# Two plain f blocks per layer, seven rounds, 16-key blocks of 128 rows, and a last round by 320 and 192 tokens

## The chip, the core and the metric

The kernel runs on one core of one Trainium2 chip. TensorE multiplies matrices into PSUM; VectorE (DVE) and ScalarE (ACT) do elementwise work, GpSimd (POOL) too but without access to PSUM; SyncE (SP) issues most DMA transfers. The engines run side by side, each in its own fixed order, and wait for one another through semaphores. The metric is the device time of one execution in microseconds (us); shorter is better.

## What is computed

The reference is two layers of a decoder. 16 learned tokens stand before the 512 tokens of the input and are dropped at the end, so a layer works on 528 columns and the last one needs 512.

```python
def hybrid_layer(h, ...):
    xn = rmsnorm(h, attn_norm_g)
    proj = jnp.einsum('bld,dc->blc', xn, w_in)
    fq, fk, fv, flog, rq, rk, rv, rg = jnp.split(proj, SPLIT_POINTS, axis=-1)
    fox_out = fox_attention(fq, fk, fv, log_sigmoid(flog + b_fgate))  # 8 heads of 64, softmax
    ret = retention_chunkwise(rotate(rq), rotate(rk), rv)             # 4 heads of 128, decay
    ret_out = jax.nn.silu(rg) * head_groupnorm(ret, ret_gn_g)
    mix = jnp.concatenate([fox_out, ret_out], axis=-1)
    h = h + jnp.einsum('blc,cd->bld', mix, w_out)
    hn = rmsnorm(h, ffn_norm_g)
    ff = jax.nn.silu(jnp.einsum('bld,df->blf', hn, w_gate)) * jnp.einsum('bld,df->blf', hn, w_up)
    return h + jnp.einsum('blf,fd->bld', ff, w_down)
```

Two such layers (D 1024, DFF 2816) and a final rmsnorm give the output. All inputs are float32.

## The kernel before

Everything is kept transposed: 128 features on the partitions, tokens along the columns. `h` is eight tiles of 128 x 528. Each product of float32 matrices is made of three fp32r matmuls: high part by high part, high by low, low by high (`split`, L119; the weights' parts are whi and wlo or fwhi and fwlo, L168, L169, L798, L799). Weights arrive by SP in tiles of 128 x 1024 (raw, three buffers; fraw, two) and are split by ScalarE and VectorE, in the attention stage mostly by ScalarE and POOL.

**Order.** The plan is a list of small steps. TensorE executes exactly in list order (`manual_schedule`, L1128). For the other engines a scheduler fixes the order when the program is built: what stands earlier in the list goes first, what isn't ready lets later work pass. `tc.high_priority()` moves instructions ahead; `keep_in_program_order` holds one behind the instruction listed before it on its engine.

**Attention.** Keys stand in five blocks: four of 128 and one of 16 (`KOFF`, `KLEN`, L561). `transpose_into` (L376) turns blocks through TensorE. For the last block the kernel uses tiles of 16 rows: the value products in `fox_steps` (L530) and `ret_steps` (L674) contract over `kn = KLEN[j]` rows, and in layer 0 the block of the 16 leading queries is turned as a 16 x 16 tile (L385).

**Feed-forward.** DFF is 22 blocks f of 128. The first `PLAIN` of a layer are plain: a gate product and an up product, each eight steps over D. Every other f is a `Unit` (L817): gate and up together as seven block products in place of eight, over two halves of the tokens. It needs sums of weight blocks (L844, L845, L851, L857) and sums of input blocks, the four **x forms** (`x_forms`, L764: scratch tile S of two buffers, results th and tl). The list places the x forms at fixed steps after the stage begins (L1024); they are needed by the first unit's `middle` (L904). A unit runs head, middle, one down product, tail, another down product. The blocks f go in rounds (`ROUNDS`); the down products of a round are the fills of the next round's units, one pair of output tiles per unit, and what no unit took follows at the round's end. Each adds its sum to `h` (L952).

**The end.** In the last layer the last round's down products run over the first half of the tokens, then over the second (`HC`, 256 and 256 columns; L997 adds to `h`). `squares_last` (L309) sums the squares of `h`, `rstd` multiplies them by ones on TensorE and forms R, `scaled` (L1041) multiplies `h` by the norm's weight on ScalarE, and `final` (L1033) multiplies by R and sends the output.

Of the kernel before, what the change touches and what calls it, by code (L numbers as in the profile page):

```python
# [16 lines left out]
NK = D // 128  # L17
# [9 lines left out]
ROUNDS = ((0, 3), (3, 7), (7, 11), (11, 15), (15, 19), (19, 22))  # L27
PLAIN = 3
# [10 lines left out]
def hybrid_kernel(ctx, tc, x_t, w_in, w_fl, w_out, w_gate, w_up, w_down, vecs, b_fg, rope, decay, mask, ident, out_t):  # L39
# [27 lines left out]
    p_tiles, pm_tiles, vt_tiles, low_keys = [], [], [], []  # L67
    rot = {"pm": 0, "vt": 0}
# [12 lines left out]
    def enter_att(l):  # L81
        enter("att")
        low_keys[:] = [phase["att"].tile([128, T], F32R, name=f"kl{s}") for s in range(2)]
        for s, t in enumerate(low_keys):
            (nc.gpsimd if l else nc.vector).memset(t[64 * (1 - s):64 * (2 - s)].bitcast(F32), 0.0)
        for lst, n, shape in ((p_tiles, NBLK, [128, TP]), (pm_tiles, 2, [META, 128]), (vt_tiles, 1, [128, T])):
            lst[:] = [phase["att"].tile(shape, F32, name=f"pd{shape[1]}_{n}_{i}") for i in range(n)]

            for i, t in enumerate(lst):
                if lst is not vt_tiles:  # L90
                    z0 = META + 128 * (i + 1) if lst is p_tiles else META
                    (nc.gpsimd if l else nc.vector).memset(t[:, z0:z0 + 128 - META], 0.0)
# [165 lines left out]
    def col_rstd(parts, n, cols, rname):  # L258
# [4 lines left out]
        for i, s in enumerate(parts):  # L263
            for v, (c0, c1) in zip(views, cols):
                nc.tensor.matmul(v, ones, s[:, c0:c1], start=(i == 0), stop=(i == len(parts) - 1))
# [43 lines left out]
    def squares_last(st, cols):  # L309
# [9 lines left out]
        sh, sl = (fft(f"tl{i}", shape=(128, T)) for i in range(2))  # L319
        sq = tt("sq")  # L320
        nc.scalar.activation(sh[:, c], h[NK - 1][:, c], AF.Square)
        nc.vector.tensor_mul(sq[:, c], h[NK - 1][:, c], h[NK - 1][:, c])
        nc.vector.tensor_sub(sl[:, c], sq[:, c], sh[:, c].bitcast(F32))
        st["parts"] = parts + (sh, sl)
# [51 lines left out]
    def transpose_into(src, offs, parts=128, last=128):  # L376


        out = []
        for j0 in range(0, len(offs), 4):  # L380
            grp = offs[j0:j0 + 4]
            ps = psum_a()
            rows = last if j0 + len(grp) == len(offs) and len(grp) == 1 else 128
            for j, o in enumerate(grp):
                nc.tensor.transpose(ps[0:rows, 128 * j:128 * j + parts], src[:, o:o + rows], idt[0:parts, 0:parts])  # L385
            out.append((j0, len(grp), rows, ps[0:rows, 0:128 * len(grp)].rearrange("p (j q) -> p j q", j=len(grp))))
        return out

    def fox_dense(l, g, ly, real, st):
# [30 lines left out]
        def v_done(ps):  # L420
            vt = take(vt_tiles, "vt")
# [10 lines left out]
    def fox_steps(g, st, ly, real):  # L432
# [5 lines left out]
        def values():  # L438
            st["v"] = [at(f"vv{s}", shape=(128, 5, 128)) for s in range(2)]
            for j0, n, rows, p3 in transpose_into(st["vt"], KOFF, last=META):  # L440
                for s in range(2):
                    v = st["v"][s][0:rows, j0:j0 + n]
# [11 lines left out]
        def scores(s, b):  # L454
# [11 lines left out]
            for c0, c1 in segs:  # L466
# [8 lines left out]
                nc.vector.tensor_tensor_reduce(pt[:, c0:c1], sc[0:nq, 0:c1 - c0], bc[0:nq, c0:c1],  # L475
# [11 lines left out]
            pr = pt[:, 0:nk]  # L487
# [16 lines left out]
        def turn(s, b):  # L504
# [6 lines left out]
            for j0, n, _, p3 in transpose_into(info[s, b], [128 * j for j in range(b + 2)], nq):  # L511
                split(pth[:, j0:j0 + n, q0:q0 + nq], ptl[:, j0:j0 + n, q0:q0 + nq], p3[:, :, 0:nq])

        def product(s):
# [11 lines left out]
            for j in range(5):  # L526
                c0 = max(0, KOFF[j] - META)
                kn = KLEN[j]
                for i, pp in enumerate(pt):
                    nc.tensor.matmul(po[:, c0:SEQ], v[0:kn, j, :], pp[0:kn, j, META + c0:T],  # L530
# [33 lines left out]
    def ret_dense(l, hd, ly, real, st, which):  # L564
# [17 lines left out]
        def v_done(ps):  # L582
            vr = at("vr", F32)
# [15 lines left out]
    def ret_steps(l, hd, st, real):  # L599
# [5 lines left out]
        def values():  # L605
# [3 lines left out]
            for j0, n, rows, p3 in transpose_into(st["vr"], KOFF, last=META):  # L609
                mn = mean[0:rows, j0:j0 + n]  # L610
                nc.vector.tensor_reduce(mn, p3, axis=mybir.AxisListType.X, op=ALU.add)
                nc.vector.tensor_scalar_mul(mn, mn, -1.0 / 128.0)
                for j in range(n):
                    nc.scalar.activation(vh[0:rows, j0 + j], p3[:, j], AF.Identity, bias=mn[:, j])
                for j in range(n):
                    nc.vector.scalar_tensor_tensor(vl[0:rows, j0 + j], p3[:, j], mn[:, j],
                                                   vh[0:rows, j0 + j].bitcast(F32), ALU.add, ALU.subtract)
# [6 lines left out]
        def scores(grp):  # L624
# [32 lines left out]
            if full < used:  # L657
                split(sh[0:kn, full:used], sl[0:kn, full:used], sd[0:kn, full:used])
            kept["t", grp[0]] = (sh, sl)

        def product(grp):
# [5 lines left out]
            for j in grp:  # L667
                used, g0 = kept[j]
                sh, sl = kept["t", g0]
                q0 = q_start(j)  # L670
                qa = max(q0, META)
                kn = KLEN[j]
                for i, (a, b) in enumerate(((vh, sh), (vh, sl), (vl, sh))):
                    nc.tensor.matmul(po[:, qa - META:SEQ], a[0:kn, j, :], b[0:kn, used + qa - q0:used + T - q0],  # L674
# [48 lines left out]
    def ffn(l, st, real, last):  # L723
# [77 lines left out]
        def product(j, o, x, bank, fresh, final, n=HB, done=None):  # L801

            def chunk(k):
                def go():
# [4 lines left out]
                    for i, (a, b) in enumerate(((hi, xh), (hi, xl), (lo, xh))):  # L809
                        nc.tensor.matmul(bank()[:, 0:w], a[:, o + k, :], b, start=(fresh and k == 0 and i == 0),  # L810
# [182 lines left out]
        else:  # L993
# [39 lines left out]
    def final(st, c0, c1, pinned=NK):  # L1033
        r = st["R"][:, c0:c1].unsqueeze(1).broadcast_to([128, 2, c1 - c0])
        for k in range(0, NK, 2):
# [167 lines left out]
```

## Time and profile before

| | before |
|---|---|
| time, median of 3 runs (lowest to highest) | 1299.45 us (1298.94 to 1300.29) |
| the profiled execution: its time, its span | 1300.5 us, 1298.7 us |
| granted TensorE clock, mean | 0.995 |
| VectorE busy in it | 1004.4 us (77%) |
| ScalarE busy in it | 706.1 us (54%) |
| HBM read, written | 116.91 MB, 2.13 MB |

The span runs from the first to the last instruction; the execution's time has some 2 us around it. PE is TensorE's matmuls and PEld its weight loads, which overlap them. A row of a group or of the timeline names line, engine, operation, tiles (out<-in) and shape; an arrow in brackets names what ended the idle time before an instruction.

### The profile page before, as it was taken

The numbers are of one execution on the slowest core, as the hardware profiler recorded it, in microseconds if no ns is written. First come the engines' busy times: TensorE is split into PE (matmuls) and PEld (weight loads), VectorE is DVE, ScalarE is ACT, GpSimd is POOL, SyncE is SP. The second block draws the span as 40 slices with busy tenths as digits, with TensorE's granted clock in tenths as the row PEclk, the third lists the DMA queues.
The fourth block names the chain that finished last, engine by engine and source line by source line (L and its number), as shares of the span: only waits on it lengthen the run. The fifth ranks groups of instructions, "written<-read, shape, count | busy, mean of one in ns | idle before, by whom it ended". The sixth has DMA issues, their size and how long they took to land.

```text
span 1298.7 us, 23288 instructions
## 1 busy us (share of the span) xinstructions
PE 1271.5 (98%) x9326; PEld 1207.8 (93%) x9326; DVE 1004.4 (77%) x1823; ACT 706.1 (54%) x1277; POOL 192.2 (15%) x153
## 2 busy tenths in 40 slices
PE   8999999999999999999999999999999999999996
PEld 7999999999999999999998989888789999999995
DVE  7877756769887888887776767567899887888866
ACT  6767545667544444444466665457664444444444
POOL 3332334230000000000023323333200000000000
PEclk9999999999999999999999999999999999999998
DMA  5322222213333333332313222222223333333321
GB/s 198 108 80 66 88 85 66 74 49 125 106 96 98 98 98 98 98 98 82 118 55 115 74 82 83 74 84 72 93 82 118 114 98 98 98 98 104 107 66 65
DMA packets 45468, 120.54 MB, mean 93 GB/s; under 512 B 5376, under 2 KB 12032, under 8 KB 45360
## 3 DMA queue, kind: packets, MB, share of 16 engines
q1 hardware_dynamic: 45120, 118.90, 29.2%
q8 instruction: 73, 1.20, 0.4%
q0 software_dynamic: 96, 0.13, 0.1%
q14 instruction: 35, 0.29, 0.1%
q10 hardware_dynamic: 144, 0.02, 0.0%
HBM read 116.91 MB, written 2.13 MB: 92 GB/s over the span
## 4 chain that ended last, share of the span: by engine, by line
PE 86%; DVE 7%; ACT 5%; issue 1%; DMA 1%; POOL 0%; SPq 0%; DVEq 0%; ACTq 0%; POOLq 0%
PE psd L192 24%; PE psa L810 18%; PE psd L945 14%; PE psd L810 13%; PE psa L192 5%; PE psa L945 4%; PE psa L385 2%; PE psa L530 1%; PE psa L674 1%; PE psa L469 1%; PE psa L647 1%; DVE xl L291 1%; ACT whi L168 1%; DVE tq L575 1%; PE psa L347 1%
## 5 line engine op out<-in xcount | busy, mean ns | idle before, releaser
L169 POOL TENSOR_TENSOR wlo<-raw,whi 128x512 fp32r<-128x512 f32 x136 | 186.5, 1387 | 400.5 <-ACT whi L168 398.3
L192 PE MATMUL psd<-xh,whi 128*128 128x264 f32 (+1 forms) x792 | 197.0, 316 | 5.0 <-ACT whi L168 5.0
L192 PE MATMUL psd<-xh,wlo 128*128 128x264 f32 (+1 forms) x792 | 187.2, 304 | 0.4 <-POOL wlo L169 0.4
L192 PE MATMUL psd<-xl,whi 128*128 128x264 f32 (+1 forms) x792 | 187.1, 304 | 0.4 <-DVE xl L291 0.4
L192 PEld LDWEIGHTS psd<-xh,whi 128*128 128x128 f32 x792 | 128.8, 190 | 9.9 <-ACT whi L168 5.0
L192 PEld LDWEIGHTS psd<-xh,wlo 128*128 128x128 f32 x792 | 127.5, 189 | 6.5 <-POOL wlo L169 0.6
L192 PEld LDWEIGHTS psd<-xl,whi 128*128 128x128 f32 x792 | 128.1, 189 | 5.2 <-DVE xl L291 1.0
L168 ACT CAST whi<-raw 128x512 fp32r<-128x512 f32 (+1 forms) x170 | 99.4, 613 | 38.8 <-issue 19.8
L798 ACT CAST whi<-raw 128x1024 fp32r<-128x1024 f32 (+2 forms) x62 | 54.8, 884 | 49.6 <-PE psd L810 37.6
L798 ACT CAST fwhi<-raw 128x1024 fp32r<-128x1024 f32 (+2 forms) x62 | 55.7, 899 | 47.2 <-PE psd L810 39.4
L799 DVE TENSOR_TENSOR wlo<-raw,whi 128x1024 fp32r<-128x1024 f32 (+2 forms) x62 | 62.9, 1015 | 11.9 <-ACT whi L798 11.7
L799 DVE TENSOR_TENSOR fwlo<-raw,fwhi 128x1024 fp32r<-128x1024 f32 (+2 forms) x62 | 64.0, 1032 | 8.8 <-ACT fwhi L798 8.6
L488 ACT ACTIVATE pd<-pd,nmax 128x144 f32<-128x144 f32 (+4 forms) x72 | 39.3, 545 | 52.7 <-DVE nmax L475 40.8
L810 PE MATMUL psa<-tl,whi 128*128 128x264 f32 (+1 forms) x232 | 65.8, 284 | 0.0
L810 PE MATMUL psa<-th,whi 128*128 128x264 f32 (+1 forms) x232 | 65.8, 284 | 0.0
L810 PE MATMUL psa<-th,wlo 128*128 128x264 f32 (+1 forms) x232 | 65.7, 283 | 0.0
L810 PE MATMUL psa<-th,fwhi 128*128 128x264 f32 (+1 forms) x224 | 63.6, 284 | 0.0
L810 PE MATMUL psa<-th,fwlo 128*128 128x264 f32 (+1 forms) x224 | 63.5, 284 | 0.0
L810 PE MATMUL psa<-tl,fwhi 128*128 128x264 f32 (+1 forms) x224 | 63.4, 283 | 0.0
L121 DVE TENSOR_TENSOR ptl<-psa,pth 128x512 fp32r<-128x512 f32 (+4 forms) x88 | 41.8, 490 | 24.2 <-ACT pth L120 23.9
L798 ACT CAST fwhi<-S 128x1024 fp32r<-128x1024 f32 x20 | 21.0, 1051 | 69.7 <-PE psa L810 66.3
L876 ACT COPY e<-psa 128x264 f32<-128x264 f32 (+1 forms) x114 | 42.8, 375 | 27.9 <-PE psa L810 23.9
(291 smaller groups left out, 4030.8 us busy)
## 6 DMA issues: line engine op xcount, KB each, us to landing
raw<-w_in SPq DMA_DIRECT2D x54, 512.0 KB, 3.5
raw<-w_gate SPq DMA_DIRECT2D x44, 512.0 KB, 3.9
fraw<-w_up SPq DMA_DIRECT2D x38, 512.0 KB, 3.5
raw<-w_down SPq DMA_DIRECT2D x64, 256.0 KB, 2.9
raw<-w_out SPq DMA_DIRECT2D x16, 512.0 KB, 3.4
raw<-w_down SPq DMA_DIRECT2D x32, 192.0 KB, 2.5
bc<-cdr SPq DMA_DIRECT2D x16, 264.0 KB, 3.5
raw<-w_up SPq DMA_DIRECT2D x6, 512.0 KB, 3.6
```

The lines of the kernel that those rows point to most:

```text
L121: nc.vector.tensor_sub(lo, src, hi.bitcast(F32))
L168: nc.scalar.copy(hi, job["raw"][:, c0:c1])
L169: sub(lo, job["raw"][:, c0:c1], hi.bitcast(F32))
L192: nc.tensor.matmul(ps[1][b][:, 0:c1 - c0], w[:, wk, :], x[:, c0:c1], start=(k == 0 and i == 0), stop=(k == n - 1 and i == 2))
L291: nc.vector.scalar_tensor_tensor(xl[:, c], h[k][:, c], g, xh[:, c].bitcast(F32), ALU.mult, ALU.subtract)
L385: nc.tensor.transpose(ps[0:rows, 128 * j:128 * j + parts], src[:, o:o + rows], idt[0:parts, 0:parts])
L488: nc.scalar.activation(pr, pr, AF.Exp, bias=nmax[0:nq], scale=-1.0, accum_out=rsum)
L798: nc.scalar.copy(hi, src)
L799: nc.vector.tensor_sub(lo, src, hi.bitcast(F32))
L810: nc.tensor.matmul(bank()[:, 0:w], a[:, o + k, :], b, start=(fresh and k == 0 and i == 0), stop=(k == n - 1 and i == 2), skip_group_check= ...
L876: nc.scalar.copy(self.t["e"][:, i], self.t["x"][:, 0:w])
L945: nc.tensor.matmul(v[:, 0:c1 - c0], a[:, s * n + k, :], b[:, c0:c1], start=(k == 0 and i == 0), stop=(k == n - 1 and i == 2))
```

## The change

It has four parts.

1. `PLAIN` goes from 3 to 2, and the 22 blocks go in seven rounds (2, 4, 4, 3, 3, 3, 3) in place of six (3, 4, 4, 4, 4, 3). One more f of each layer is a unit.
2. The 16-key block is padded with zeros to 128 rows: two value tiles of 640 columns (`v_tiles`), the 16-query tiles of 128 rows (`pm_tiles`), and small tiles `end_tiles` for the retention block's scores, zeroed once when the attention stage of a layer is entered. Products and transposes of that block then use 128 rows.
3. The last round runs over 320 and then 192 columns. The first part's norm is now `squares`, the full one, and its `scaled` stands right behind its `rstd`.
4. `squares_last`, for the second part, sums six squares in place of seven, gives h6's square to TensorE as float32 without a split, and puts its additions ahead by priority. `final` and `scaled` are called in pieces with some of them pinned.

```diff
-ROUNDS = ((0, 3), (3, 7), (7, 11), (11, 15), (15, 19), (19, 22))
-PLAIN = 3
+ROUNDS = ((0, 2), (2, 6), (6, 10), (10, 13), (13, 16), (16, 19), (19, 22))
+PLAIN = 2
...
+        for lst, n, cols, z0 in ((p_tiles, NBLK, TP, None), (v_tiles, 2, TP, T)):
+            lst[:] = [phase["att"].tile([128, cols], F32, name=f"pd{z0}_{i}") for i in range(n)]
...
+        pm_tiles[:] = [phase["att"].tile([128, 128], F32, name=f"pm{i}") for i in range(2)] if l == 0 else []
+        for t in pm_tiles:
+            zero(l, t)
+        end_tiles[:] = [[phase["att"].tile([128, META], F32R, name=f"rs{i}{k}") for k in range(2)] for i in range(2)]
+        for t in end_tiles[0] + end_tiles[1]:
+            zero(l, t.bitcast(F32))
+
+    def zero(l, t):
+        (nc.gpsimd if l else nc.vector).memset(t, 0.0)
...
-                nc.tensor.matmul(v, ones, s[:, c0:c1], start=(i == 0), stop=(i == len(parts) - 1))
+                nc.tensor.matmul(v, ones if s.dtype == F32R else ones.bitcast(F32), s[:, c0:c1], start=(i == 0), stop=(i == len(parts) - 1))
...
-        for k in range(NK - 1):
+        for k in range(NK - 2):
             sq = tt("sq") if k else acc
             nc.scalar.activation(sq[:, c], h[k][:, c], AF.Square)
             if k:
-                nc.vector.tensor_add(acc[:, c], acc[:, c], sq[:, c])
-        parts = col_parts(acc, cols)
...
+                with tc.high_priority():
+                    nc.vector.tensor_add(acc[:, c], acc[:, c], sq[:, c])
+        hi, lo = col_parts(acc, cols)
+        one = fft("S", F32, (128, T), 2)
...
+        nc.scalar.activation(one[:, c], h[NK - 2][:, c], AF.Square)
         nc.scalar.activation(sh[:, c], h[NK - 1][:, c], AF.Square)
...
+        st["parts"] = (hi, one, lo, sh, sl)
...
-                nc.tensor.transpose(ps[0:rows, 128 * j:128 * j + parts], src[:, o:o + rows], idt[0:parts, 0:parts])
+                nc.tensor.transpose(ps[:, 128 * j:128 * j + 128], src[:, o:o + 128], idt)
...
-                    nc.tensor.matmul(po[:, c0:SEQ], v[0:kn, j, :], pp[0:kn, j, META + c0:T],
+                    nc.tensor.matmul(po[:, c0:SEQ], v[:, j, :], pp[:, j, META + c0:T],
...
+                eh, el = end_tiles[hd % 2]
+                split(eh[0:kn], el[0:kn], sd[0:kn, full:used])
...
+                if j == 4:
+                    (sh, sl), used = kept["e"], 0
                 for i, (a, b) in enumerate(((vh, sh), (vh, sl), (vl, sh))):
-                    nc.tensor.matmul(po[:, qa - META:SEQ], a[0:kn, j, :], b[0:kn, used + qa - q0:used + T - q0],
+                    nc.tensor.matmul(po[:, qa - META:SEQ], a[:, j, :], b[:, used + qa - q0:used + T - q0],
...
-            for c0, c1 in HC:
+            LC = ((t0, t0 + 320), (t0 + 320, T))
+            for c0, c1 in LC:
...
-            places = [(end, lambda: squares_last(fin[0], HC[0:1])),
-                      (end + 9, lambda: rstd(fin[0], HC[0:1], "r")),
-                      (2 * end, lambda: squares_last(fin[1], HC[1:2])),
-                      (2 * end, lambda: scaled(fin[1], *HC[1])),
-                      (2 * end, lambda: scaled(fin[0], *HC[0])),
-                      (2 * end, lambda: final(fin[0], *HC[0], NK // 2)),
-                      (2 * end, lambda: rstd(fin[1], HC[1:2], "R")),
-                      (2 * end, lambda: final(fin[1], *HC[1]))]
+            places = [(end, lambda: squares(fin[0], LC[0:1])),
+                      (end + 9, lambda: rstd(fin[0], LC[0:1], "r")),
+                      (end + 9, lambda: scaled(fin[0], *LC[0], 0, NK)),
+                      (2 * end, lambda: scaled(fin[1], *LC[1], 0, NK - 1)),
+                      (2 * end, lambda: squares_last(fin[1], LC[1:2])),
+                      (2 * end, lambda: final(fin[0], *LC[0], HB, NK)),
+                      (2 * end, lambda: scaled(fin[1], *LC[1], NK - 1, NK)),
+                      (2 * end, lambda: final(fin[0], *LC[0], 0, HB)),
+                      (2 * end, lambda: rstd(fin[1], LC[1:2], "R")),
+                      (2 * end, lambda: final(fin[1], *LC[1], 0, NK))]
...
+    def final(st, c0, c1, k0, k1):
...
+        for k in range(k0, k1, 2):
+            y = st["y"][k // HB][:, k % HB:k % HB + 2]
+            mul = nc.vector.tensor_mul(y, y, r)
+            if k0:
                 tc.keep_in_program_order(mul)
```

More of the change, by code (lines that the diff above doesn't have):

```diff
@@ L382, in transpose_into @@
             ps = psum_a()
[L383 removed]
             for j, o in enumerate(grp):
[L385 to L386 removed]
+                nc.tensor.transpose(ps[:, 128 * j:128 * j + 128], src[:, o:o + 128], idt)
+            out.append((j0, len(grp), ps[:, 0:128 * len(grp)].rearrange("p (j q) -> p j q", j=len(grp))))
         return out
@@ L420, in v_done @@
         def v_done(ps):
-            vt = take(vt_tiles, "vt")
+            vt = v_tiles[0]
             for t, (c0, c1) in zip(ps, FULL):
@@ L439, in values @@
             st["v"] = [at(f"vv{s}", shape=(128, 5, 128)) for s in range(2)]
-            for j0, n, rows, p3 in transpose_into(st["vt"], KOFF, last=META):
+            for j0, n, p3 in transpose_into(st["vt"], KOFF):
                 for s in range(2):
-                    v = st["v"][s][0:rows, j0:j0 + n]
+                    v = st["v"][s][:, j0:j0 + n]
                     a0, a1 = ROWS[s]
@@ L608, in values @@
             mean = tmp.tile([128, 5, 1], F32, name="mean", tag="mean")
-            for j0, n, rows, p3 in transpose_into(st["vr"], KOFF, last=META):
-                mn = mean[0:rows, j0:j0 + n]
+            for j0, n, p3 in transpose_into(st["vr"], KOFF):
+                mn = mean[:, j0:j0 + n]
                 nc.vector.tensor_reduce(mn, p3, axis=mybir.AxisListType.X, op=ALU.add)
@@ L809, in go @@
                     for i, (a, b) in enumerate(((hi, xh), (hi, xl), (lo, xh))):
-                        nc.tensor.matmul(bank()[:, 0:w], a[:, o + k, :], b, start=(fresh and k == 0 and i == 0),
+                        nc.tensor.matmul(bank()[:, 0:b.shape[-1]], a[:, o + k, :], b, start=(fresh and k == 0 and i == 0),
                                          stop=(k == n - 1 and i == 2), skip_group_check=not (fresh and final))
```

63 lines of the change are left out of this document (31 added, 32 removed).

## The prediction

> **What bounds the kernel now.** I read the head of the page first, then the busy time by windows, then single stretches of the timeline. In the page: the span, and the busy us of each engine with its share of it.
>
> ```profile
> span 1298.7 us, 23288 instructions
> ...
> PE 1271.5 (98%) x9326; PEld 1207.8 (93%) x9326; DVE 1004.4 (77%) x1823; ACT 706.1 (54%) x1277; POOL 192.2 (15%) x153
> ```
>
> TensorE is the bound, so an edit is worth the TensorE time it removes unless another engine then comes late. The windows (columns: stretch, length, busy us of PE, PEld, DVE, ACT, POOL, granted clock, DMA share, GB/s) show where one could:
>
> ```profile
> 60.00:90.00 30.00, 30.00 (x240) 29.42 (x240) 21.74 (x45) 21.36 (x43) 7.92 (x6) 1.00 0.29 88
> 315.00:330.00 15.00, 15.00 (x125) 14.84 (x124) 15.00 (x26) 8.40 (x12) 0.00 (x0) 1.00 0.24 66
> 400.00:500.00 100.00, 100.00 (x823) 100.00 (x822) 81.24 (x121) 43.23 (x61) 0.00 (x0) 1.00 0.32 99
> 955.00:970.00 15.00, 15.00 (x67) 12.19 (x66) 15.00 (x26) 8.23 (x12) 0.00 (x0) 1.00 0.32 98
> 1284.00:1299.00 15.00, 1.96 (x9) 1.28 (x7) 8.60 (x19) 3.22 (x9) 0.00 (x0) 0.63 0.40 138
> ```
>
> The attention stage (first row) has VectorE at 72%: TensorE alone decides. The feed-forward rounds (third) have VectorE at 81%. But at the **start of the feed-forward stage** of each layer (second and fourth rows) VectorE is busy 15.00 of 15.00 us while TensorE does not yet wait. The last row is the tail, where TensorE has nothing left.
>
> **16-key blocks of 128 rows.** Weight loads (start, us, engine, line, tiles, rows * columns) around three 16-row products (L674):
>
> ```profile
> 79.37 0.19 PEld L674 LDWEIGHTS psa<-rsh,rvl 128*128 128x128 f32 x1
> 79.64 0.18 PEld L674 LDWEIGHTS psa<-rsh,rvh 16*128 16x128 f32 x1
> 79.75 0.18 PEld L674 LDWEIGHTS psa<-rsl,rvh 16*128 16x128 f32 x1
> 79.86 0.19 PEld L674 LDWEIGHTS psa<-rsh,rvl 16*128 16x128 f32 x1
> 80.06 0.30 PEld L192 LDWEIGHTS psd<-xh,whi 128*128 128x128 f32 x2
> 80.29 0.19 PEld L192 LDWEIGHTS psd<-xl,whi 128*128 128x128 f32 x1
> ```
>
> The same behind a 128-row product that also has 16 columns (L679):
>
> ```profile
> 70.69 0.19 PEld L679 LDWEIGHTS psa<-rsh,rvl 128*128 128x128 f32 x1
> 70.80 0.30 PEld L192 LDWEIGHTS psd<-xh,whi 128*128 128x128 f32 x2
> 71.03 0.19 PEld L192 LDWEIGHTS psd<-xl,whi 128*128 128x128 f32 x1
> ```
>
> With 128 rows one load starts 0.11 us after the other (70.69, 70.80). Going from 128 rows to 16 takes 0.27 (79.37 to 79.64), and back 0.20 (79.86 to 80.06). With 128 rows the five loads after 79.37 would come at 79.48, 79.59, 79.70, and then, as behind 70.69, 0.34 later the one that now stands at 80.29: at 80.04. So a group saves 0.25 us, whether it has two or three products. By the code there are 16 groups at L530 (four pairs of heads, two heads, two layers) and 8 at L674 (four heads, two layers); layer 0 also has 8 transposes of a 16-row block at L385, of which one that stands alone looks so:
>
> ```profile
> 118.23 0.31 PEld L192 LDWEIGHTS psd<-xh,wlo 128*128 128x128 f32 x2
> 118.68 0.13 PEld L385 LDWEIGHTS psa<-idt,pd 16*128 16x128 f32 x1
> 118.84 0.30 PEld L192 LDWEIGHTS psd<-xh,whi 128*128 128x128 f32 x2
> 119.07 0.19 PEld L192 LDWEIGHTS psd<-xl,whi 128*128 128x128 f32 x1
> ```
>
> 24 groups by 0.25 are 6.0 us. A lone transpose saves 0.24 (119.07 would be 118.83: loads at 118.35, 118.47 and 118.59, then 0.24). Where a transpose follows a group directly, as here, the switch is counted already:
>
> ```profile
> 60.04 0.18 PEld L530 LDWEIGHTS psa<-ptl,vv 16*128 16x128 f32 x1
> 60.17 0.13 PEld L385 LDWEIGHTS psa<-idt,pd 16*128 16x128 f32 x1
> ```
>
> That is so for three of the eight; five by 0.24 are 1.2. Together **7.2 us**. I take 6.3, since a few TensorE waits in attention end on other engines and would eat some; the range is 4.5 to 7.2. The other edits of this part I cost at nothing: copies and subtractions of 128 partitions instead of 16 in the values, and four more small memsets a layer (POOL's in layer 1, queued ahead of its first weight subtraction). VectorE's and POOL's slack in the first window hides them. The transposes of the values still load and stream once per block.
>
> The Trainium skill, "TensorE: Matmul & The Clock Gate", Why this matters for your kernels, says that a matmul over 32 rows takes the same time as one over 128. The loads inside the 16-row group agree (0.11 apart), but the rule has no price for the switch that the rows above show; by the rule alone this part would bring 0.
>
> **Two plain blocks instead of three.** Chain of waits (start, us, what), each row a stretch without a gap:
>
> ```profile
> 316.98 17.58 PE psd L192 x144
> ...
> 955.76 16.64 PE psd L192 x72
> ...
> 1267.08 11.66 PE psa L810 x99
> ```
>
> A matmul takes 0.122 us at 264 columns, 0.231 at 512 and 0.118 at 256. A plain f has 96 of 264 in layer 0; a unit (seven products instead of eight) has 84: 12 by 0.122 are 1.47 us saved. In layer 1, 48 by 0.231 (11.09) against 84 by 0.118 (9.91): 1.18. Together **-2.65**.
>
> But the first unit now starts 96 by 0.122 = 11.7 us (layer 0) and 11.1 us (layer 1) sooner after the stage begins, while the four x forms stay at their places in the list and VectorE is full there. Layer 1 before, VectorE and the first matmul of the first unit:
>
> ```profile
> 976.31 0.69 DVE L799 TENSOR_TENSOR wlo<-raw,whi 128x512 fp32r<-128x512 f32 x1
> ...
> 979.13 1.23 DVE L799 TENSOR_TENSOR fwlo<-raw,fwhi 128x1024 fp32r<-128x1024 f32 x1 [0.21 <-ACT fwhi L798]
> ```
>
> ```profile
> 972.23 0.28 PE L810 MATMUL psa<-xh,whi 128*128 128x256 f32 x1
> ```
>
> VectorE has its first idle 0.21 us at 979.13, so it can be counted by work. Everything the first unit needs up to its first down product is done at 976.31. Away falls what belongs to the third plain f: four weight halves and four elementwise operations of 512 columns, which follow one another at 0.60, so 4.8; also 0.3 for a smaller w_down tile and 0.6 for a subtraction that can wait. That leaves 970.6. The down product starts 7.1 us into the unit (five products of 12 by 0.118), so at 979.3 before and at 968.2 now: VectorE is **2.4 us late at the least**. Layer 0, counted alike:
>
> ```profile
> 339.10 0.69 DVE L799 TENSOR_TENSOR wlo<-raw,whi 128x512 fp32r<-128x512 f32 x1
> 342.52 0.69 DVE L844 TENSOR_TENSOR S<-fraw 128x512 f32<-128x512 f32 x1 [2.74 <-DMA fraw<-w_up]
> ```
>
> ```profile
> 334.39 0.28 PE L810 MATMUL psa<-xh,whi 128*128 128x264 f32 x1
> ```
>
> 339.1 less 4.8, 0.3, 0.6 and 1.8 (sums for the next unit done early) is 331.6, needed at 341.7 - 11.7 = 330.0: 1.6 late. That is the best order. In list order the fourth x form stands behind the unit's second and third weights, and it is needed by the middle products, about 4 us into the unit (965.1, and 326.8). If VectorE takes it last of this work but the w_down tile, TensorE waits to 970.0 and 331.0: 4.9 and 4.2 us. The ends are 4.0 and 9.1 for both layers. I take the middle, **+6.5**: nothing in the rows says which order is built. A pure saving (0) I exclude as the likeliest by the count. Later units with two-f fills take 84 by 0.122 plus 24 by 0.122 = 13.2 us, against some 12.4 of VectorE (81.24 per 100 at 132 matmuls or 16 us a unit, less 0.6): close, but I cost them at nothing.
>
> **Seven rounds.** The down products stay 22 x 8 steps a layer, so TensorE is unchanged. Each layer gets eight additions to h of 0.69 us and eight more w_down transfers on SP's queue. VectorE's 19% in the third window hides the additions, and the DMA share there is 0.32.
>
> **Last round.** 72 matmuls go from 256 to 320 columns and 72 from 256 to 192. By the two widths in the rows, 320 takes 0.118 + 64 x 0.00044 = 0.146: +2.0 us. 192 columns by that slope would take 0.090, but each matmul brings a load, and loads are 0.11 apart at best (70.69, 70.80): I take 0.111, -0.5 us; the slope's end is -2.0. Two fewer norm matmuls, -0.2. A first-half norm that now squares and splits all eight tiles may come 0 to 0.5 us late: +0.2. Sum +1.5.
>
> The Trainium skill, same page, Back-to-back issue gap, gives columns / 2.4 + 2.5 ns for an isolated matmul, 82 ns at 192; by it the second half would be 2.1 us shorter than I take it. The loads above speak for the other number, and no row here has 192 columns.
>
> The tail before:
>
> ```profile
> 1284.20 0.28 PE L810 MATMUL psa<-ah,fwlo 128*128 128x256 f32 x1
> 1288.56 0.58 PE L265 MATMUL psa<-sqh,ones 128*128 128x256 f32 x1 [4.07 <-ACT sqh L120]
> ```
>
> ```profile
> 1290.06 0.47 ACT L270 ACTIVATE R<-psa,epsc 128x256 f32<-128x256 f32 x1 [1.56 <-PE psa L265]
> ```
>
> ```profile
> 1292.39 2.50 DVE L1036 TENSOR_TENSOR th<-th,R 128x512 f32<-128x512 f32 x4
> ```
>
> From the last matmul to the end are 14.5 us: 4.4 to the norm's matmuls (VectorE carries the first half's outputs among the sums), 1.5 for them, 2.3 to R, 2.5 for the outputs, 3.8 for the last transfer. After: the sums have priority and two outputs are pinned behind them, 192 columns shorten each step, and h6's square goes to TensorE unsplit. I estimate 2.3, 1.5, 2.1, 2.0 and 3.6, that is 11.5: -3.0. The unsplit matmul in full fp32 is in no row; between one matmul (0.12) and four at the slow clock's 0.58 it costs 0.1 to 2.3; I take 0.4 within the 1.5. Together the last round is **-1.5**, between -4 and +1.
>
> **Rivals.** (a) *VectorE keeps up*: the x forms and weights come in the best order, waits 0 to 4.0. Against it: the full windows. Time 6.3 + 2.65 + 1.5 less 0 to 4.0 faster: 1289 to 1293. (b) *VectorE becomes the bound at both starts, slower*: the x form comes last, its scratch tile S (two buffers) is also taken by the unit's sums, and the weights behind it follow late. Each start then waits some 2 us more than with the x form last, a cast and a subtraction of an S tile (1.23 at 979.13, and about as much on ScalarE): 13 in all. It decides from 10.5 us of waits, where all savings (6.3 + 2.65 + 1.5) are spent; at 13 with a tail worth nothing the time is 1303.5. For it: two stretches at 15.00 of 15.00; against it: the count needs only 4.0. (c) *The rows do not matter*, the page's rule above: no 6.3, so 1302. Against it: 0.27 and 0.20 where 0.11 would do. (d) *The tail is not shorter*, its 3.0 lost: 1298.5.
>
> **The numbers.** -6.3 - 2.65 + 6.5 - 1.5 = **-3.95** us. Against the profiled execution (span 1298.7, 1300.5 in all) that is a span of 1294.75 and 1296.55; the median of the runs is 1.05 below that execution, so **1295.5**. Chances: forecast 0.45 (own range 1292.5 to 1298.5), (a) 0.25, (b) 0.15, (c) 0.08, (d) 0.07. 0.2% is 2.6 us, about what a measurement of this kernel can tell from no change. Of the forecast 0.31 lies beyond it on the fast side and 0.14 within; (a) is fast; (b) 0.12 slow, 0.03 within; (c) and (d) 0.05 slow, 0.09 within, 0.01 fast. So faster 0.57, same 0.26, slower 0.17. The range 1288 to 1303 leaves out the ends of (a) and (b).
>
> **What would show it.** Right: no 16-row product left, and loads 0.11 apart at those places; TensorE's first gap in each feed-forward stage at the first unit's middle products, ended by VectorE's tl or wlo, 1.6 to 6 us long; matmuls of 320 at 0.146 and of 192 at 0.11; last matmul to end 11 to 12 us. Wrong: no such gap ((a)), gaps beyond 5 us in each layer ((b)), or attention as long as before ((c)).

## The result and the profile after

The changed kernel takes **1317.93 us** (median of 4 runs, 1315.55 to 1317.98) against 1299.24 us for the kernel before (4 runs, 1298.94 to 1300.29): 18.7 us slower, a ratio of 1.0134 (95% interval 1.0122 to 1.0146). The forecast was 1295.5 in a range of 1288 to 1303. The head of the page:

```profile
span 1316.1 us, 23453 instructions
...
PE 1275.8 (97%) x9350; PEld 1212.4 (92%) x9350; DVE 1023.1 (78%) x1866; ACT 712.6 (54%) x1291; POOL 192.7 (15%) x157
```

TensorE's share of the span went from 98% to 97%: it waits. To see where, the span is cut at the first product of each stage, here in TensorE's timeline of the changed kernel (start, us, engine, line, tiles, shape):

```profile
300.03 0.41 PE L200 MATMUL psd<-xh,whi 128*128 128x264 f32 x2
...
666.50 0.39 PE L200 MATMUL psd<-xh,whi 128*128 128x512 f32 x1
...
944.63 0.39 PE L200 MATMUL psd<-xh,whi 128*128 128x512 f32 x1
...
1302.05 0.27 PE L823 MATMUL psa<-ah,fwlo 128*128 128x192 f32 x1
```

and of the kernel before, whose last product starts at 1284.20:

```profile
298.97 0.41 PE L192 MATMUL psd<-xh,whi 128*128 128x264 f32 x2
...
657.30 0.39 PE L192 MATMUL psd<-xh,whi 128*128 128x512 f32 x1
...
938.49 0.39 PE L192 MATMUL psd<-xh,whi 128*128 128x512 f32 x1
```

The same cuts in the profiles of the parts run alone (experiments 1 to 3) stand beside them, in us (each row is the difference of two neighbouring starts):

| stage | before | after | rows_only | plain_only | last_only |
|---|---|---|---|---|---|
| attention, layer 0 | 298.97 | 300.03 | 297.28 | 300.54 | 299.82 |
| feed-forward, layer 0 | 358.33 | 366.47 | 358.34 | 367.38 | 358.35 |
| attention, layer 1 | 281.19 | 278.13 | 278.49 | 279.76 | 279.87 |
| feed-forward, layer 1, to the last product | 345.71 | 357.42 | 345.60 | 355.45 | 348.24 |
| from there to the end | 14.52 | 14.10 | 14.50 | 14.48 | 14.09 |

From before to after the rows differ by +1.06, +8.14, -3.06, +11.71 and -0.42, together the 17.4 us of the spans. The two feed-forward stages carry the loss. TensorE's timeline at the first unit of layer 0, the idle time and what ended it in brackets:

```profile
328.49 0.28 PE L823 MATMUL psa<-th,fwlo 128*128 128x264 f32 x1
332.55 0.59 PE L823 MATMUL psa<-th,fwhi 128*128 128x264 f32 x1 [3.77 <-ACT th L128]
333.94 0.59 PE L823 MATMUL psa<-tl,fwhi 128*128 128x264 f32 x1 [0.81 <-DVE tl L129]
334.33 0.42 PE L823 MATMUL psa<-th,fwlo 128*128 128x264 f32 x1
334.55 0.42 PE L823 MATMUL psd<-th,fwhi 128*128 128x264 f32 x1
```

These are the middle products, waiting for the fourth x form, as forecast. New is what follows: matmuls of 264 columns start 0.22 us apart (334.33, 334.55) where they had started 0.12 apart. The windows of the same stretch (columns as in the prediction) say why:

```profile
334.00:336.00 2.00, 2.00 (x9) 2.00 (x10) 2.00 (x4) 0.38 (x1) 0.00 (x0) 0.50 0.22 20
```

```profile
326.00:342.00 16.00, 10.98 (x64) 10.26 (x64) 13.26 (x21) 5.36 (x9) 0.00 (x0) 0.79 0.28 82
```

The granted clock is 0.50 behind the wait. 0.79 over 16 us is 16 x 0.21 / 0.5 = 6.7 us at half clock. Layer 1 shows the same at its first unit:

```profile
976.77 0.58 PE L823 MATMUL psa<-th,fwhi 128*128 128x256 f32 x1 [4.44 <-ACT th L128]
```

Counted from start to start, the matmuls of these two stretches take 8.4 and 8.3 us more than their usual spacing of 0.122 and 0.118 would, 16.8 in all. That is the largest part of the change, and not the whole: savings stand against it, and smaller losses beside it (see below). VectorE and ScalarE ahead of the wait:

```profile
326.39 1.21 DVE L812 TENSOR_TENSOR fwlo<-S,fwhi 128x1024 fp32r<-128x1024 f32 x1
...
328.14 1.21 DVE L812 TENSOR_TENSOR wlo<-fraw,whi 128x1024 fp32r<-128x1024 f32 x1
...
330.90 0.48 DVE L788 SCALAR_TENSOR_TENSOR S<-h,vec,S 128x264 f32<-128x264 f32 x1
...
332.63 1.25 DVE L129 TENSOR_TENSOR tl<-S,th 128x1056 fp32r<-128x1056 f32 x1
```

```profile
331.42 1.07 ACT L128 CAST th<-S 128x1056 fp32r<-128x1056 f32 x1 [2.53 <-DVE S L788]
```

VectorE splits the unit's second and third weights (326.39, 328.14) and only then finishes the fourth form (330.90). That is the order of the list: by the code the two plain blocks are steps 0 to 31, the unit's head begins at step 32 and asks for three weight tiles at once, and the fourth form stands at step 36.

### The profile page after: what moved, and what is told of

Read it like the earlier page. It is cut to its first block, busy times and chain, and to the rows that moved or that the text cites. A ratio compares the mean times of both kernels' runs of the same rounds, so it can differ in the third digit from the quotient of the medians.

```text
span 1316.1 us, 23453 instructions
## 1 busy us (share of the span) xinstructions
PE 1275.8 (97%) x9350; PEld 1212.4 (92%) x9350; DVE 1023.1 (78%) x1866; ACT 712.6 (54%) x1291; POOL 192.7 (15%) x157
## 4 chain that ended last, share of the span: by engine, by line
PE 75%; DVE 15%; ACT 7%; issue 2%; DMA 1%; SPq 0%; DVEq 0%; ACTq 0%
PE psd L200 18%; PE psa L823 17%; PE psd L958 14%; PE psd L823 13%; PE psa L200 4%; PE psa L958 3%; PE psa L396 2%; PE psa L480 1%; DVE xl L299 1%; ACT whi L176 1%; DVE ss L314 1%; PE psa L540 1%; PE psa L657 1%; PE psa L687 1%; DVE tq L585 1%
## 5 line engine op out<-in xcount | busy, mean ns | idle before, releaser
L200 PE MATMUL psd<-xh,whi 128*128 128x264 f32 (+1 forms) x744 | 184.4, 316 | 5.0 <-ACT whi L176 5.0
L200 PE MATMUL psd<-xh,wlo 128*128 128x264 f32 (+1 forms) x744 | 174.6, 303 | 0.4 <-POOL wlo L177 0.4
L200 PE MATMUL psd<-xl,whi 128*128 128x264 f32 (+1 forms) x744 | 174.6, 303 | 0.2 <-DVE xl L299 0.2
L200 PEld LDWEIGHTS psd<-xh,whi 128*128 128x128 f32 x744 | 121.5, 191 | 8.5 <-ACT whi L176 5.0
L200 PEld LDWEIGHTS psd<-xh,wlo 128*128 128x128 f32 x744 | 120.0, 190 | 5.8 <-POOL wlo L177 0.6
L200 PEld LDWEIGHTS psd<-xl,whi 128*128 128x128 f32 x744 | 120.5, 190 | 3.9 <-DVE xl L299 0.7
L823 PE MATMUL psa<-th,whi 128*128 128x264 f32 (+1 forms) x256 | 73.1, 285 | 0.0
L958 PE MATMUL psd<-ah,fwhi 128*128 128x264 f32 (+1 forms) x254 | 71.8, 331 | 0.3 <-DVE sg L899 0.3
L958 PE MATMUL psd<-ah,fwlo 128*128 128x264 f32 (+1 forms) x254 | 71.1, 329 | 0.0
L958 PE MATMUL psd<-al,fwhi 128*128 128x264 f32 (+1 forms) x254 | 70.8, 327 | 0.0
```

The costliest lines, as they stand in the source:

```text
L200: nc.tensor.matmul(ps[1][b][:, 0:c1 - c0], w[:, wk, :], x[:, c0:c1], start=(k == 0 and i == 0), stop=(k == n - 1 and i == 2))
L823: nc.tensor.matmul(bank()[:, 0:b.shape[-1]], a[:, o + k, :], b, start=(fresh and k == 0 and i == 0), stop=(k == n - 1 and i == 2), skip_gr ...
L958: nc.tensor.matmul(v[:, 0:c1 - c0], a[:, s * n + k, :], b[:, c0:c1], start=(k == 0 and i == 0), stop=(k == n - 1 and i == 2))
```

## The experiments

Every time is a median; "before" was timed on the same chip beside each group of runs (1299.3 to 1300.0). The cuts are those of the table above.

| run | us (lowest to highest) | ratio to before, 95% interval |
|---|---|---|
| rows_only | 1297.26 (1296.02 to 1297.74) | 0.9977 (0.9968 to 0.9987) |
| plain_only | 1318.03 (1316.97 to 1319.41) | 1.0138 (1.0124 to 1.0152) |
| last_only | 1302.14 (1301.10 to 1303.59) | 1.0018 (1.0009 to 1.0027) |
| fill | 1312.84 (1310.90 to 1316.87) | 1.0108 (1.0092 to 1.0124) |
| forms_early | 1311.31 (1310.80 to 1312.00) | 1.0086 (1.0072 to 1.0100) |
| forms_pool | 1319.33 (1317.18 to 1320.29) | 1.0146 (1.0132 to 1.0160) |
| forms_light | 1311.69 (1310.64 to 1313.22) | 1.0090 (1.0076 to 1.0104) |
| early_light | 1304.30 (1303.26 to 1306.87) | 1.0038 (1.0025 to 1.0052) |
| six_rounds | 1319.65 (1317.49 to 1321.46) | 1.0150 (1.0136 to 1.0164) |
| tail_order | 1316.31 (1315.75 to 1318.73) | 1.0128 (1.0115 to 1.0142) |
| rows_sums_first | 1296.47 (1295.80 to 1299.37) | 0.9976 (0.9964 to 0.9987) |
| rows_outputs_last | 1295.44 (1294.32 to 1296.84) | 0.9966 (0.9952 to 0.9979) |

**1 to 3. Each part alone, on the kernel before.** The edits are the parts of the diff: `rows_only` has the padded tiles, `plain_only` the two lines of ROUNDS and PLAIN, `last_only` the parts 3 and 4.

> The kernel before with part 2 alone: the 16-key block padded to 128 rows. Theory (the switch costs 0.25 us each and is gone, and the changed kernel lost it in layer 0 only through waits near 131 to 135 us behind which the granted clock fell to half): 6.3 us less, 1290 to 1295, each switch gone as steps of 0.2 to 0.25 us; if the half clock at 135 us returns, about 3 less in layer 1 alone, 1295 to 1297. Rival (the longer form of the copies makes layer 0's attention longer by itself): 2 us less at most, 1297 to 1299, with new waits spread over layer 0. Rival (rows do not matter): no change.

> The kernel before with part 1 alone: two plain blocks a layer and seven rounds. Theory (the first unit of each layer waits 6 to 7 us for the fourth x form, then runs 2 us longer at half clock; rounds of three add some 1 us of waits per layer): 16 us more, 1313 to 1318. Rival (the waits come from the parts together): 1299 to 1305, as the sum in the prediction had it for this part, +3.9.

> The kernel before with parts 3 and 4 alone: the last round by 320 and 192 columns and the norm in pieces. Theory (in the sums for the second norm, ScalarE scales a tile before it squares it and VectorE adds each square before the next h, a chain of 1.4 us a tile, and the norm's matmuls wait for h6's square): about 2.8 us more, 1301 to 1303. Rival (this was late only because the round before it was): 1.5 us less, 1296 to 1299.

Against the 1299.73 beside them they measured -2.5, +18.3 and +2.4, sum +18.2: the parts add up to the change, and plain_only carries it, with the same wait at the same product. The waits for th are 3.77 and 4.44 us there and not the 6 to 7 that were expected. The rows bring less than half of what was reckoned. Their 1297.26 lies just above the theory's last range and in that of the rival with the longer copies; but that rival makes layer 0's attention longer, and it became 1.7 us shorter (298.97 to 297.28).

**4. The half clock.** Useless matmuls keep TensorE busy in the wait of the first unit (the added lines; `middle` then returns `a` and its other two products):

```diff
+                def extra():
+                    for _ in range(32):
+                        nc.tensor.matmul(y()[:, 0:w], ones, xs(0)[0][:, t0:t0 + w], start=True, stop=True)
+                a = product(self.w2, 0, t_form(2), x, False, False, done=self.keep(1))
+                if self.f == PLAIN:
+                    a.insert(HB - 1, extra)
```

> The changed kernel with 32 matmuls more in each layer, put ahead of the fourth x form's first product of the first unit, into a bank whose next product starts afresh. They need nothing that is late. Theory (the half clock behind the wait comes from TensorE standing idle): TensorE is busy in the wait, the granted clock stays at 1.00 there, the 26 or so matmuls behind it take 0.12 in place of 0.22, and the kernel takes 4 us less, 1312 to 1315. Rival (the slow matmuls have another cause, such as VectorE's traffic at that place): no change or slower, 1317 to 1320, with the clock at 0.5 as before.

TensorE's timeline there:

```profile
325.94 4.18 PE L922 MATMUL psd<-xh,ones 128*128 128x264 f32 x32
329.95 0.30 PE L823 MATMUL psa<-th,fwhi 128*128 128x264 f32 x1
331.26 0.39 PE L823 MATMUL psa<-tl,fwhi 128*128 128x264 f32 x1 [1.00 <-DVE tl L129]
331.49 0.28 PE L823 MATMUL psa<-th,fwlo 128*128 128x264 f32 x1
331.61 0.28 PE L823 MATMUL psd<-th,fwhi 128*128 128x264 f32 x1
```

```profile
325.00:335.00 10.00, 9.00 (x72) 8.79 (x71) 9.30 (x14) 3.92 (x6) 0.00 (x0) 1.00 0.44 131
```

The form is as late as before, but the clock stays at 1.00 and the products start 0.12 apart (331.49, 331.61). The two feed-forward stages take 363.70 and 355.63, 2.8 and 1.8 less than in the changed kernel. So the half clock comes from the idle time, and costs 4.6 us of the 16.8. (The four runs of fill spread over 6 us; the stages of the one profile carry this reading.)

**5 to 8. Why the fourth form is late: order or amount.** Four edits of the x forms in the changed kernel. forms_early puts all four ahead of the unit in the list:

```diff
-            steps.insert(NK + 4 + 9 * i, x_forms(i))
+            steps.insert(NK + 4 + 5 * i, x_forms(i))
```

> The changed kernel with the x forms five places apart in the list in place of nine, so that all four stand ahead of the first unit. Theory (VectorE has too much work ahead of the unit in whatever order; what is late is only exchanged): the wait for th goes, the unit's second weights then come 3 to 4 us late in its place, and the time lies within 3 us of the changed kernel's, 1314 to 1319, lower by up to 5 where the wait is too short for the half clock. Rival (the order in the list alone makes the wait): waits of some 2 us a layer at full clock, 9 to 10 us less, 1306 to 1309.

```profile
328.46 0.39 PE L823 MATMUL psa<-th,fwhi 128*128 128x264 f32 x1 [2.18 <-ACT fwhi L811]
329.74 0.59 PE L823 MATMUL psa<-th,fwlo 128*128 128x264 f32 x1 [0.77 <-DVE fwlo L812]
```

TensorE waits 2.18 us for the second weights' high part and 0.77 for their low part in place of the form, and the clock still falls, for some 3.4 us in place of 6.7. 6.6 us less: between the two expectations.

forms_pool moves the additions to GpSimd (the added lines; two of the unit's `t_form` calls change with them, since two sums change places):

```diff
+                nc.scalar.activation(s[:, 4:6], two(h[HB + k]), AF.Copy, scale=g1)
+                nc.gpsimd.tensor_sub(s[:, 2], s[:, 1], s[:, 0])
+                nc.gpsimd.tensor_sub(s[:, 3], s[:, 5], s[:, 1])
+                nc.gpsimd.tensor_sub(s[:, 5], s[:, 5], s[:, 2])
+                nc.gpsimd.tensor_sub(s[:, 4], s[:, 4], s[:, 5])
```

> The changed kernel with the x forms' four additions each moved from VectorE to GpSimd, which does nothing in that stage, and the scaling of the second row of blocks to ScalarE. VectorE has 6.4 us less to do ahead of the first unit of each layer. Theory (VectorE's amount of work makes the wait): the waits at the first units and the half clock behind them go but for 1 us a layer, 13 to 15 us less, 1303 to 1306. Rival (the chain of one x form, or GpSimd's slower additions, sets the time): a wait of 3 us or more remains in each layer, 1309 to 1318.

Nothing was gained: 1319.33 is above both expectations, and with runs from 1317.18 not clear of the changed kernel. A line of VectorE's timeline and two of GpSimd's in that run:

```profile
321.42 1.78 DVE L812 TENSOR_TENSOR fwlo<-S,fwhi 128x1024 fp32r<-128x1024 f32 x1
```

```profile
320.20 0.75 POOL L785 TENSOR_TENSOR S<-S 128x264 f32<-128x264 f32 x1 [4.33 <-ACT S L783]
320.90 1.21 POOL L786 TENSOR_TENSOR S<-S 128x264 f32<-128x264 f32 x1
```

The split that took 1.21 at 326.39 above takes 1.78 beside GpSimd, and GpSimd's subtraction 0.75 to 1.21. Over the first 30 us of layer 0's stage the instructions that VectorE has in both kernels take 6.3 us more, as much as it was to be spared. The waits for th at the first units are gone, but TensorE waits elsewhere, longest 4.7 us in the stage's plain products. The profile puts that wait down to ScalarE's S (L783), which this product does not read; VectorE's sg (L759), which empties a bank of psd, ends at the same time, 320.1. Which of them held it isn't shown.

forms_light leaves GpSimd out and takes 4.7 us from VectorE by giving ScalarE the low parts, as plain copies. It leaves out the subtraction that makes them low parts, so it and early_light are probes of time and don't compute the layer:

```diff
-                split(th, tl, s[:, 2:6])
+                nc.scalar.copy(th, s[:, 2:6])
+                nc.scalar.copy(tl, s[:, 2:6])
```

> The changed kernel, but ScalarE writes the x forms' low parts as plain copies in place of VectorE's subtractions, so the low parts hold the values and not the differences. VectorE has four instructions of 1.17 us, 4.7 us, less to do ahead of the first unit of each layer, and GpSimd stays idle. Theory (the amount of VectorE's work ahead of the first unit makes the wait, and GpSimd took from VectorE what it was to give): the wait for th falls from 4 us to about 1, under what the half clock needs, and 10 to 14 us go, 1304 to 1308. Rival (the chain of one x form sets it, whatever VectorE has to do): waits of 3 us or more and the half clock stay, 1312 or more.

```profile
328.44 0.39 PE L824 MATMUL psa<-th,fwhi 128*128 128x264 f32 x1 [2.14 <-ACT th L790]
```

6.2 us less, a miss for both: the wait for th is 2.1 us in layer 0 in place of 3.8, and 3.6 in layer 1 in place of 4.4, and the form still stands behind the third weights. Amount and place each explain a part. Together:

> The edits of forms_early and forms_light together: the x forms five places apart, their low parts plain copies by ScalarE (values, not differences). Each alone left about 10 us of the 17. Theory (the wait has two causes that add up, 4.7 us a layer of VectorE's work and the place of the last form behind the unit's weights): waits of at most 1.5 us a layer and the clock at 1.00, 1302 to 1306. Rival (a third engine's queue, ScalarE's, takes over): waits of 2 us or more a layer remain, 1308 to 1312.

```profile
326.49 0.39 PE L824 MATMUL psa<-th,fwhi 128*128 128x264 f32 x1 [0.77 <-ACT e L890]
326.72 0.29 PE L824 MATMUL psa<-tl,fwhi 128*128 128x264 f32 x1
327.96 0.39 PE L824 MATMUL psa<-th,fwlo 128*128 128x264 f32 x1 [0.95 <-DVE fwlo L813]
```

No wait at the first units reaches 1 us, none is for the form, and the granted clock there is 1.00. 13.6 us of the changed kernel's time are gone. So both causes are real, and with both lifted the change still doesn't pay: 1304.3 is above before.

**9. Rounds.** `ROUNDS` of 2, 4, 4, 4, 4, 4 in the changed kernel.

> The changed kernel with two plain blocks as it has, but rounds of 2, 4, 4, 4, 4 and 4 in place of seven. Theory (rounds of three cost a few waits of 0.1 to 0.5 us where a round ends, 1.8 us in all beyond the first units, and a third of the unit's cover): 1 to 2 us less than the changed kernel, 1315.5 to 1317; the last round is then a third longer, so its part of the change is the same. Rival (the seven rounds cost nothing): no change, 1317 to 1319.

1319.65 is above both expectations; against the before beside each it is 19.6 us in place of 18.7, and the runs of the two kernels overlap, so no gain is all that the times show. The traces show an exchange. With rounds of three, matmuls come late every three units, some 49 us apart (547 and 596, then 1184, 1233 and 1283 us in the changed kernel); six_rounds has none of that, but a longer wait at the end of each layer's last round. TensorE in plain_only, then in six_rounds:

```profile
548.88 0.51 PE L945 MATMUL psd<-ah,fwhi 128*128 128x264 f32 x2 [0.73 <-DVE sg L886]
```

```profile
642.76 0.51 PE L958 MATMUL psd<-ah,whi 128*128 128x264 f32 x2 [2.06 <-ACT ah L128]
...
1277.80 0.41 PE L823 MATMUL psa<-ah,whi 128*128 128x320 f32 x1 [2.95 <-ACT ah L128]
```

Counted against the usual spacing, all late starts beyond the first units come to 3.5 us in plain_only and 2.8 in the changed kernel (without its last round). Before has none but 0.2 at 317 us, which the others show too and which is not counted here. In six_rounds the two places above alone take 2.8 and 3.8. By the code a round of three units leaves one pair of the fills over, which then stands between the last unit and the products that need it, and a round of four leaves none. That this makes the wait for ah is argued, not shown.

**10. The end.** tail_order exchanges two lines:

```diff
-                      (2 * end, lambda: scaled(fin[1], *LC[1], 0, NK - 1)),
                       (2 * end, lambda: squares_last(fin[1], LC[1:2])),
+                      (2 * end, lambda: scaled(fin[1], *LC[1], 0, NK - 1)),
```

> The changed kernel with two lines of the end exchanged: the second part's squares stand ahead of its scaling, so ScalarE squares a tile of h before it scales it. Theory (the chain h, scale, square, sum of 1.4 us a tile holds the norm's matmuls, and h6's square is late by the scaling): 0.4 us less for each of four tiles, 1.5 to 2 us less than the changed kernel, 1315.5 to 1317, and the norm's first matmul within 2.6 us of the last product. Rival (VectorE's outputs of the first part among the sums set it): no change.

ScalarE of the changed kernel, and TensorE in both (tail_order second):

```profile
1303.99 0.46 ACT L1066 ACTIVATE tl<-h,gf 128x192 f32<-128x192 f32 x1 [0.69 <-DVE h L1010]
1304.35 0.35 ACT L323 ACTIVATE sq<-h 128x192 f32<-128x192 f32 x1
```

```profile
1305.52 0.53 PE L273 MATMUL psa<-sqh,ones 128*128 128x192 f32 x1 [3.20 <-ACT sqh L128]
1306.92 1.01 PE L273 MATMUL psa<-S,ones 128*128 128x192 f32 x2 [0.87 <-ACT S L332]
```

```profile
1303.78 0.35 PE L273 MATMUL psa<-sqh,ones 128*128 128x192 f32 x1 [2.63 <-ACT sqh L128]
1304.84 0.65 PE L273 MATMUL psa<-S,ones 128*128 128x192 f32 x2 [0.70 <-ACT S L332]
```

Each square had waited behind a scaling of 0.46. The wait ahead of the norm falls from 3.20 to 2.63, and from the last product to the end it is 13.1 us in place of 14.1. That 1.0 us is what the trace shows; the medians differ by 1.6, but the runs of the two kernels overlap. The norm's first matmul starts 2.9 us behind the last product, not within the 2.6 that were expected, so the scaling was a part of the delay and not all of it.

**11 and 12. A faster kernel.** The rows of 128 with before's blocks and last round, and the sums of squares by priority; rows_outputs_last also holds all four outputs of the first half behind the sums:

```diff
-                nc.vector.tensor_add(acc[:, c], acc[:, c], sq[:, c])
+                with tc.high_priority():
+                    nc.vector.tensor_add(acc[:, c], acc[:, c], sq[:, c])
...
-                      (2 * end, lambda: final(fin[0], *HC[0], NK // 2)),
+                      (2 * end, lambda: final(fin[0], *HC[0], 0)),
```

> The kernel before with the 16-key block on 128 rows and, of the change to the end, only the priority for the sums of squares; the last round stays at 256 and 256 columns. One output of the first part less stands among the sums. Theory (VectorE's order holds the last norm): 0.6 us less than rows_only, 1296 to 1297. Rival (the squares of ScalarE hold it): as rows_only, 1297 to 1297.5.

> As rows_sums_first, and all four outputs of the first part stand behind the sums, in VectorE's wait for the norm. Theory: the norm's first matmul comes about 3 us behind the last product in place of 4.4, 1.5 us less than rows_only, 1295 to 1296.5, the fastest version. Rival (the outputs' transfers then run into those of the second part): no gain, 1297 to 1299.

```profile
1280.15 0.28 PE L819 MATMUL psa<-ah,fwlo 128*128 128x256 f32 x1
1282.60 0.38 PE L273 MATMUL psa<-sqh,ones 128*128 128x256 f32 x1 [2.17 <-ACT sqh L128]
```

2.5 us from the last product to the norm, where it was 4.4, and 12.6 from that product to the end, where it was 14.5. The norm's matmul takes 0.38 in place of before's 0.58: behind the shorter wait it runs at the full clock. 1295.44 is 4.6 us below the before timed beside it, a third of a percent, and the lowest median of all; its runs overlap those of rows_sums_first.

## Why the prediction was wrong

**Two plain blocks: the step that failed.** The saving of 2.65 us, the shift of 11 us, the place (middle products of each first unit) and the late tile were right. Wrong was "I take the middle, +6.5: nothing in the rows says which order is built". The list says it: the forms stand at fixed steps, the fourth behind the start of the head, which fetches three weight tiles, and the order built was the list's. The waits for th, 3.8 and 4.4 us, are near the 4.2 and 4.9 that the prediction had for that order, and smaller waits (tl, the weights, a bank) add 1.3 a layer. That makes rival (b), which had 13 us, the nearest. To (b) too one term was missing: TensorE at half clock behind the wait, 4.6 us by experiment 4. The trace of before had shown it: the tail's window quoted in the prediction has a clock of 0.63, and the norm's matmuls there take 0.58. The prediction priced that clock in the tail and not behind the wait it forecast itself. Measured, the term +6.5 is 16.8: 8.2 of waits for th, 2.6 of smaller ones, 4.6 of half clock, and 1.4 that these runs don't take apart. (The 1303.5 that the prediction gives for (b) leaves out both the round's +1.5 and the tail's -3.0; with the tail worth nothing, as it says, its own terms make 1305.0.) That order and amount both make the form late is shown by forms_early, forms_light and early_light. The count (1.6 us late at the least in layer 0) was a fair lower bound: forms_early, with the order mended and all the work left, waits 2.18 and 0.77 us there.

**Rows: right mechanism, size off.** Rival (c) falls: loads now stand 0.11 apart at these places, and in 20 of the 24 groups the product behind the group comes 0.21 to 0.23 us sooner after the one ahead of it than in before, near the 0.25 reckoned. But 6.3 us became 2.5. In layer 1 attention takes 278.49 in rows_only against 279.76 and 279.87 in the two runs without the rows: 1.3 of the 3 reckoned (12 groups by 0.25). The switch was priced rightly; what was mis-sized is what comes behind it. TensorE that comes sooner waits longer for others. In layer 0 of before and then of after:

```profile
132.32 0.28 PE L679 MATMUL psa<-rsh,rvh 128*128 128x16 f32 x1 [0.40 <-DVE ptl L121]
...
135.28 0.66 PE L538 MATMUL psa<-idt,tq 128*128 128x128 f32 x4 [0.24 <-ACT d L680]
```

```profile
132.16 0.28 PE L692 MATMUL psa<-rsh,rvh 128*128 128x16 f32 x1 [0.82 <-DVE ptl L129]
...
135.58 0.69 PE L548 MATMUL psa<-idt,tq 128*128 128x128 f32 x2 [0.76 <-ACT d L693]
```

Two waits took back 0.94 us here. "A few TensorE waits would eat some" was priced at 0.9 for both layers; these two alone take that. All TensorE waits up to the feed-forward stage and in layer 1's attention together go from 14.3 us in before to 15.8 in rows_only; where the rest of the shortfall went was not traced. Behind this spot the changed kernel's profile also has the clock at half, and its layer 0 shows +1.06 where rows_only shows -1.7:

```profile
130.00:145.00 15.00, 13.21 (x78) 12.46 (x77) 9.69 (x18) 6.63 (x15) 3.88 (x3) 0.77 0.27 89
```

In rows_only, with waits of the same length:

```profile
130.00:145.00 15.00, 13.15 (x100) 12.41 (x100) 10.55 (x19) 8.15 (x19) 4.71 (x4) 1.00 0.29 89
```

The eleven profiles with the rows sort by this clock: up to the feed-forward stage they take 296.9 to 297.8 us where it is 1.00 here (six), 298.5 to 299.0 at 0.89 (four) and 300.0 at 0.77 (the changed kernel). Of the three without the rows one has the fall (plain_only). Whether the rows make it more frequent stays open. And the 3.1 us that layer 1 seems to gain from before to after are partly a fall of the same kind in before's profile (clock 0.96 from 760 to 800 us), since attention there takes 281.19 in it and 279.8 in the two other runs without the rows.

**Last round.** As reckoned, 320 columns take 0.146 us and 192 take 0.11 (18 products in 2.63 and 1.99); the +1.5 became +2.5 in last_only through waits for additions to h (0.66 us ahead of the last tile in the changed kernel's profile). **The tail** was to give 3.0 and gave 0.42. Of its five steps three held (R 2.0, outputs 2.0, transfer 3.6). The first, 2.3, is 3.5: the new order put ScalarE's scaling ahead of each square, which the diff shows and the prediction didn't follow through. That is half of the miss, since tail_order has 2.9; the other half stays open. The second, 1.5, is 3.0, since h6's square came last and TensorE waited for it. Rival (d) came near; with the round, parts 3 and 4 cost 2.4 where -1.5 was forecast.

**Seven rounds** were put at nothing, and that did not hold. VectorE's 19% of slack is a mean over a window; the late starts of experiment 9 stand every three units, and where a wait is recorded there VectorE ends it. Whether the eight more additions to h are what makes VectorE late isn't shown. With these starts plain_only adds up: 17.6 at its first units (8.7 and 8.9, counted in the same way), 3.5 of late starts, less the 2.65 saved, is 18.4, and 18.3 was measured.

## What to carry to other kernels

Work that is taken from the bound engine uncovers what it had hidden: one matmul block of 11 us in each layer was the cover of VectorE's preparation, and was worth more than the 2.65 us that taking both away saves. If a forecast contains a TensorE wait of several us, add what the clock does behind it, and read the order of a late producer from the list rather than take a mean over orders. A saving made at many small places in a stage full of short waits was worth less than half its sum here.

## What the runs showed of the hardware

- **The clock falls in fixed portions, also where no long wait stands.** 0.77 over 15 us is 15 x 0.23 / 0.5 = 6.9 us at half clock, 0.79 over 16 us is 6.7, and 0.89 over 15 us (tail_order, at the same place) 3.3: one or two portions of 3.4. The Trainium skill, "TensorE: Matmul & The Clock Gate", What's actually happening, names a free-running window of 3413 ns; these rows agree. At 131 to 136 us no single wait is longer than 0.83 us (in plain_only 0.39), and the clock falls in some executions and stays in others with the same waits. The row is tail_order's:

```profile
130.00:145.00 15.00, 14.00 (x97) 13.26 (x96) 10.90 (x19) 7.68 (x17) 4.18 (x4) 0.89 0.29 89
```

- **GpSimd and VectorE slow one another** in float32 additions and subtractions of two tiles (1.21 to 1.78 and 0.75 to 1.21 above); VectorE's sg (L759), which reads one of its tiles from PSUM, takes 0.70 in both kernels. The Trainium skill, "SBUF — State Buffer", Who interferes with whom, describes a port pair that one of the two holds while the other waits; the rows agree with a mutual delay, but don't show which instruction held it.
